# A hybrid convolution and attention layer on one core: the first three weight chunks taken k by k with the modulation, and the output product in 512 columns

## The chip, the cores and the metric

The kernel runs on one core of a Trainium2 chip. The metric is device time in microseconds (us), the median of the runs shown. A profile of one execution, taken by the hardware profiler, stands beside it; all times of single instructions are from that execution. The engines are TensorE (PE, with its weight loads as PEld), VectorE (DVE), ScalarE (ACT), GpSimd (POOL) and SyncE (SP), whose queue issues the transfers.

## What is computed

One layer over 512 latent tokens of width 1024, with 256 context tokens. Cut to what matters here:

```
sh, sc, gt = split(silu(c) @ w_mod + b_mod)        # three vectors of 1024
h  = rmsnorm(x, pre_g) * (1 + sc) + sh             # 512 x 1024
hc = rmsnorm(ctx, pre_g) * (1 + sc_c) + sh_c       # same with c_ctx
parts = split(h @ w_in)      # b, c, x_in, z_a (conv) | q, k, v, z_b (attention) | g_a, g_b
y_a = (silu(z_a) * b * conv3(c * x_in)) @ w_out_conv
y_b = (silu(z_b) * neighbourhood_attention(q, k, v, k_ctx, v_ctx)) @ w_out_attn
y = (sigmoid(g_a) * y_a + sigmoid(g_b) * y_b) @ w_o
out = x + gt * rmsnorm(y, post_g)
```

All data are float32.

## The kernel before, in words

**Split products.** Each operand of a large product is split in two parts in a shorter format, a high part H (a cast on ACT) and a low part L (a subtraction on DVE): `split`. A product is then three matmuls per k (128 of the 1024 input channels): H by H, H by the low part of the activations, L by H. `step_T` issues them (lines 107 to 109) with weights as the stationary operand and 512 tokens as columns; `proj_N` (lines 120 to 122) has the activations stationary and 256 weight columns moving.

**Weights.** They come in chunks of 1024 x 256 (two units of 128 columns). `load_chunk` reads a chunk in two halves into two `raw` buffers and splits them into `wH` and `wL`, two buffers of each. `Chunks` loads one chunk ahead of the one in use, in the order of a hand-written plan. The order in which engines take their instructions is otherwise set by a scheduler that goes by the order of the program and by when data are ready.

**First stage.** x is loaded in four tiles of 128 tokens, normed (`normed`: sum of squares on ACT, Sqrt, reciprocal and scaling on DVE), and turned on TensorE into eight tiles of 128 channels by 512 tokens, all eight PSUM banks being used; each is drained by ACT with the gain pre_g. For each k, `load_slab` loads two slabs of w_mod (each 128 x 1024, 512 KB); `condition` forms the scale and the shift of these 128 channels as two sums over a slab on DVE (line 249); `modulate` applies them on ACT in place (line 257) and splits the result into `hx`. Chunks 0 to 2 give six units with one accumulator each. `more` brings one of them in at each of k = 0, 1, 2 and `steps` then catches up on earlier k. Four of the eight k of chunk 0 are taken as float32 (line 288), the other four are split (line 291). Chunk 3 is loaded ahead at k = 6.

**Conv stage.** The first conv outputs are formed from the six accumulators, chunk 3 follows, then `conv(2)` and `conv(3)` with four more chunks (each yields after a unit). After each unit, `modulate_c` does one k of the context's modulation (two sums on DVE, two slabs of w_mod, of which those of k = 5 to 7 are still there).

**Attention, merge, output.** Attention follows with the other projections filled in between its blocks. In the merge loop (j = 0 to 7) each j takes a chunk of the two branch projections, sums them into `mg[j]`, splits it, and works out two gates for j + 2. `post_gain` runs in this loop at j = 5 to 7: it reads c again, reads the last eight slabs of w_mod, forms eight sums (line 600), and turns the result into a row `gpost` (line 612). The output stage takes w_o in four chunks of 256 columns. For each chunk and each of four token tiles come 24 matmuls, a sum of squares on ACT (line 661) and a multiplication with `gpost` on DVE (line 662). After the last chunk the norm, the residual (line 677) and the store follow.

Of the kernel before, what the change touches and what calls it, by code (L numbers as in the profile page):

```python
# [15 lines left out]
P = 128  # L16
D = 1024
# [10 lines left out]
def layer(ctx: ExitStack, tc, xp, ctxt, cc, wmod, small, win, wout, wo, rel, tab, out):  # L28
# [22 lines left out]
    nc.vector.memset(eps, EPS)  # L51
    hcv = const.tile([P, 32], F32, name="hcv")
    cosin = const.tile([P, 2, S], F32, name="cosin")

# [23 lines left out]
    def load_chunk(src, pool=wp, raws=wp):  # L78
        H = pool.tile([P, KT, 256], F32R, name="wH", bufs=2 if pool is wp else 1)
        L = pool.tile([P, KT, 256], F32R, name="wL", bufs=2 if pool is wp else 1)  # L80
        for i in range(2):
            s = slice(4 * i, 4 * i + 4)
            raw = raws.tile([P, 4, 256], F32, name="raw", bufs=2)
            nc.sync.dma_start(raw, src[:, s])
            split(H[:, s], L[:, s], raw)
        return H, L

    class Chunks:
# [5 lines left out]
        def load(self, n, *pools):  # L94
            if n < len(self.srcs) and n not in self.ahead:
                self.ahead[n] = load_chunk(self.srcs[n], *pools)
# [53 lines left out]
    order += [wo[c] for c in range(4)]  # L150
# [53 lines left out]
    with ExitStack() as p0:  # L204
# [8 lines left out]
        def normed(xt, n, vec):  # L213
            junk = st.tile([P, D], F32, name="junk")
            ss = const.tile([P, 1], F32, name=f"ss{n}")
            if vec:
                nc.vector.tensor_tensor_reduce(
                    out=junk, in0=xt, in1=xt, scale=1.0, scalar=0.0, op0=ALU.mult, op1=ALU.add, accum_out=ss
                )
            else:  # L220
                nc.scalar.activation(junk, xt, AF.Square, accum_out=ss)
            nc.scalar.activation(ss, ss, AF.Sqrt, bias=eps, scale=1.0 / D)
            nc.vector.reciprocal(ss, ss)
            nc.vector.tensor_scalar(out=xt, in0=xt, scalar1=ss, scalar2=None, op0=ALU.mult)

# [18 lines left out]
        def condition(k, v):  # L244

            cols[k, v] = st.tile([P, 2], F32, name=f"col{v}", bufs=4)
            for i in range(2):
# [12 lines left out]
        accs = Banks(5, 0, 1, 2, 3, 4)  # L260
        acc, ws = [], []

        def more(n):
            if n:
                chunk.load(n, wp)
                ws.append(chunk.ahead[n])
            else:

                w = st.tile([P, 4, 256], F32, name="w0")
                H = st.tile([P, 4, 256], F32R, name="wH0")  # L270
                L = st.tile([P, 4, 256], F32R, name="wL0")
                nc.sync.dma_start(w, chunk.srcs[0][:, :4])
                raw = wp.tile([P, 4, 256], F32, name="raw")
                nc.sync.dma_start(raw, chunk.srcs[0][:, 4:])
                split(H, L, raw)
                ws.append((w, H, L))
            acc.extend(accs() for i in range(2))

        def steps(ks, us):
            for k in ks:  # L280
                for i in us:
                    if i >= 2:
                        step_T(acc[i], ws[i // 2], i % 2, hx, k)
                        continue
                    w, H, L = ws[0]
                    cs = slice(i * P, (i + 1) * P)
                    if k < 4:
                        nc.tensor.matmul(acc[i], lhsT=w[:, k, cs], rhs=xnT[k], start=k == 0, stop=False)
                    else:
                        for lhs, rhs in ((H, hx[0][k]), (H, hx[1][k]), (L, hx[0][k])):  # L290
                            nc.tensor.matmul(
                                acc[i], lhsT=lhs[:, k - 4, cs], rhs=rhs, start=False, stop=k == KT - 1 and lhs is L
                            )


        ones = const.tile([1, P], F32, name="ones")
        nc.vector.memset(ones, 1.0)
        crow = hp.tile([1, 2, S], F32, name="crow", tag="a0")
        nc.sync.dma_start(crow, cc[0:1].rearrange("o (a n) -> o a n", a=2))
        nc.sync.dma_start(sp, small)  # L300
        xn = [load_x(xp, i, f"x{i}", f"u{i}", hp) for i in range(4)]
        load_slab(0)
        bsc1 = const.tile([P, KT], F32, name="bsc1")
        nc.vector.tensor_scalar(out=bsc1, in0=sp[:, BM + 8:BM + 16], scalar1=1.0, scalar2=None, op0=ALU.add)
        nc.vector.tensor_scalar(out=hcv, in0=sp[:, CW:CW + 32], scalar1=0.5, scalar2=None, op0=ALU.mult)
        nc.scalar.activation(crow, crow, AF.Silu)
        nc.scalar.activation(const.tile([P, 1], F32, name="dummy"), eps, AF.Sqrt)

        for i in range(2):
            ps = tps()  # L310
            nc.tensor.matmul(ps, lhsT=ones, rhs=crow[:, i], start=True, stop=True)
            nc.vector.tensor_copy(cb[:, 0, i * S:(i + 1) * S], ps)
        xnT = halves("a")
        every = Banks(7, 0, 1, 2, 3, 4, 5, 6)
        tp = [every() for k in range(KT)]
        for i in range(4):
            normed(xn[i], f"x{i}", False)
            for k in range(KT):
                nc.tensor.transpose(tp[k][:, i * P:(i + 1) * P], xn[i][:, k * P:(k + 1) * P], ident)
        condition(0, 0)  # L320

        def drained(k):
            nc.scalar.activation(xnT[k], tp[k], AF.Identity, scale=sp[:, PG + k:PG + k + 1])

        drained(0)
        u = halves("u")
        for k in range(KT):
            if k:
                load_slab(k)
                condition(k, 0)  # L330
            modulate(k, 0, xnT[k], hx[0][k], hx[1][k])
            for i in ((1, 2, 3), (4, 5, 6, 7))[k] if k < 2 else ():
                drained(i)
            if k == KT - 1:
                nc.sync.dma_start(cb[:, 1], cc[1:2].broadcast_to([P, D]))
                nc.scalar.activation(cb[:, 1], cb[:, 1], AF.Silu)
            if k < 3:
                more(k)
            if k == 6:
                chunk.load(3, st)  # L340
            steps((k,), range(min(2 * k, 6)))
            if k < 3:
                steps(range(k + 1), (2 * k, 2 * k + 1))
        chunk.n = 3
        cn = [load_x(ctxt, i, f"c{i}", f"a{2 + i}", hp) for i in range(2)]
        for i in range(2):
            normed(cn[i], f"c{i}", i % 2)
# [6 lines left out]
        for k in range(KT):  # L354
            turned(ctT[k], cn, k)
# [405 lines left out]
```

## Time and profile before

| | us |
|---|---|
| median of 3 runs | 752.48 |
| lowest, highest | 749.15, 752.82 |
| profiled execution, time | 751.83 |
| profiled execution, span (first to last instruction) | 749.9 |

The span is what the profile divides into; the time of the same execution is 1.93 us longer. An engine's busy time is not its useful work: matmuls are pipelined, so two that follow each other overlap in the records, and the distance between their starts is what one costs. A wait is the idle time of an engine ahead of an instruction, with the instruction that ended it.

### The profile page before, as it was taken

The page shows a single profiled execution, that of the slowest core. Times are in us where ns is not written, and L with a number is a line of the kernel's source. Part 1 is how long each engine was busy: PE and PEld are TensorE (multiplying, and loading weights), DVE is VectorE, ACT ScalarE, POOL GpSimd, SP SyncE. Part 2 cuts the span into 40 slices and gives each one's busy share as a digit, 9 for nine tenths or more (in the row PEclk, how much of TensorE's full clock was granted, in tenths as well). Part 3 has the DMA queues.
Part 4 walks back from the last instruction along what each step waited for, and adds up shares of the span by engine and source line. Part 5 has one row for each costly group of instructions (what it writes and reads, how often), then busy time and mean ns, then how long its engine had stood idle before and what let it go on. Part 6 is the DMA issues. An engine that isn't in the chain of part 4 may idle for free.

```text
span 749.9 us, 10146 instructions
## 1 busy us (share of the span) xinstructions
PE 728.8 (97%) x3924; PEld 623.4 (83%) x3924; DVE 508.3 (68%) x1031; ACT 333.6 (44%) x602; POOL 0.7 (0%) x6
## 2 busy tenths in 40 slices
PE   5889999999999999999999999999999999999996
PEld 3568889888889888988889988888888888888896
DVE  4778993698796977958969678675753323338434
ACT  7666442354364544534636435534722222231422
POOL 0000000000000000000000000000000000000000
PEclk9999999999999999999999999999999999999999
DMA  8883842123211221221221222222133233348413
GB/s 327 287 312 125 297 156 97 57 71 110 73 50 64 68 102 57 72 71 67 88 99 44 80 75 71 79 88 74 58 112 110 71 101 113 107 150 302 142 57 113
DMA packets 25682, 86.16 MB, mean 115 GB/s; under 512 B 2977, under 2 KB 3489, under 8 KB 25634
## 3 DMA queue, kind: packets, MB, share of 16 engines
q1 hardware_dynamic: 25634, 85.51, 33.2%
q8 instruction: 31, 0.51, 0.3%
q14 instruction: 17, 0.14, 0.1%
HBM read 83.40 MB, written 2.10 MB: 114 GB/s over the span
## 4 chain that ended last, share of the span: by engine, by line
PE 87%; DMA 5%; DVE 5%; issue 1%; SPq 1%; ACT 1%; DVEq 0%; ACTq 0%
PE ps L107 20%; PE ps L109 20%; PE ps L108 20%; PE ps L120 5%; PE ps L122 5%; PE ps L121 5%; PE ps L499 4%; PE ps L484 4%; PE ps L453 3%; DMA wm<-in_wmod 2%; DMA wg<-in_wmod 1%; DVE junk L600 1%; DVE wL L71 1%; PE ps L462 1%; DMA raw<-in_win 1%
## 5 line engine op out<-in xcount | busy, mean ns | idle before, releaser
L107 PE MATMUL ps<-h,wH 128*128 128x512 f32 x560 | 223.6, 400 | 0.0
L109 PE MATMUL ps<-h,wL 128*128 128x512 f32 x560 | 219.6, 393 | 0.0
L108 PE MATMUL ps<-h,wH 128*128 128x512 f32 x560 | 219.5, 392 | 0.0
L70 ACT CAST wH<-raw 128x1024 fp32r<-128x1024 f32 x103 | 106.7, 1050 | 158.7 <-PE ps L108 137.6
L71 DVE TENSOR_TENSOR wL<-raw,wH 128x1024 fp32r<-128x1024 f32 x103 | 125.1, 1219 | 64.8 <-ACT wH L70 60.2
L107 PEld LDWEIGHTS ps<-h,wH 128*128 128x128 f32 x560 | 105.8, 189 | 22.9 <-ACT wH L70 1.3
L109 PEld LDWEIGHTS ps<-h,wL 128*128 128x128 f32 x560 | 105.3, 188 | 23.3 <-issue 0.7
L108 PEld LDWEIGHTS ps<-h,wH 128*128 128x128 f32 x560 | 105.9, 189 | 21.5 <-DVE h L71 0.4
L476 ACT ACTIVATE pt<-ps,m 128x512 f32<-128x512 f32 x64 | 44.1, 690 | 43.8 <-DVE m L473 43.5
L469 DVE CUSTOM_DVE_ANT_1 ps<-ps,bt 128x512 f32<-128x512 f32 x56 | 38.8, 694 | 22.6 <-PE ps L453 19.3
L70 ACT CAST TH<-ps 128x512 fp32r<-128x512 f32 x64 | 37.1, 586 | 19.8 <-PE ps L484 19.5
L71 DVE TENSOR_TENSOR TL<-ps,TH 128x512 fp32r<-128x512 f32 x64 | 43.5, 681 | 0.9
L120 PE MATMUL ps<-wH,mg 128*128 128x256 f32 x128 | 37.2, 290 | 1.8 <-ACT mg L73 1.8
L484 PE MATMUL ps<-ident,pt 128*128 128x128 f32 x256 | 38.2, 272 | 0.4 <-DVE pt L478 0.4
L120 PE MATMUL ps<-wH,h 128*128 128x256 f32 x128 | 36.9, 288 | 0.0
L121 PE MATMUL ps<-wL,mg 128*128 128x256 f32 x128 | 36.9, 288 | 0.0
L122 PE MATMUL ps<-wH,mg 128*128 128x256 f32 x128 | 36.7, 288 | 0.0
L484 PEld LDWEIGHTS ps<-ident,pt 128*128 128x128 f32 x256 | 31.0, 140 | 6.6 <-issue 0.6
L121 PE MATMUL ps<-wL,h 128*128 128x256 f32 x128 | 36.2, 283 | 0.0
L122 PE MATMUL ps<-wH,h 128*128 128x256 f32 x128 | 36.2, 283 | 0.0
L631 DVE SCALAR_TENSOR_TENSOR g<-g,ps 128x512 f32<-128x512 f32 x16 | 10.9, 684 | 35.7 <-PE ps L109 35.7
L478 DVE TENSOR_SCALAR pt<-pt,z 128x512 f32<-128x512 f32 x64 | 30.9, 483 | 1.3
(158 smaller groups left out, 1257.1 us busy)
## 6 DMA issues: line engine op xcount, KB each, us to landing
raw<-in_win SPq DMA_DIRECT2D x79, 512.0 KB, 3.6
wm<-in_wmod SPq DMA_DIRECT2D x26, 512.0 KB, 7.3
raw<-in_wout SPq DMA_DIRECT2D x16, 512.0 KB, 4.5
bt<-in_rel SPq DMA_DIRECT2D x16, 256.0 KB, 2.6
wg<-in_wmod SPq DMA_DIRECT2D x8, 512.0 KB, 4.6
raw<-in_wo SPq DMA_DIRECT2D x8, 512.0 KB, 4.1
x<-in_xp SPq DMA_DIRECT2D x4, 512.0 KB, 5.2
xr<-in_xp SPq DMA_DIRECT2D x4, 512.0 KB, 8.8
```

The lines of the kernel that those rows point to most:

```text
L70: nc.scalar.copy(H, src)
L71: nc.vector.tensor_sub(L, src, H.bitcast(F32))
L107: nc.tensor.matmul(ps, lhsT=H[:, k, cs], rhs=mH[k], start=k == 0, stop=False)
L108: nc.tensor.matmul(ps, lhsT=H[:, k, cs], rhs=mL[k], start=False, stop=False)
L109: nc.tensor.matmul(ps, lhsT=L[:, k, cs], rhs=mH[k], start=False, stop=k == KT - 1)
L120: nc.tensor.matmul(ps, lhsT=mH[k][:, ts], rhs=H[:, k], start=k == 0, stop=False)
L121: nc.tensor.matmul(ps, lhsT=mH[k][:, ts], rhs=L[:, k], start=False, stop=False)
L122: nc.tensor.matmul(ps, lhsT=mL[k][:, ts], rhs=H[:, k], start=False, stop=k == KT - 1)
L469: nc.vector.tensor_tensor_reduce(out=s3, in0=s3, in1=bt[:, e::4 - e][:, 0:2], scale=1.0, scalar=-3.0e38, op0=ALU.add, op1=ALU.max, accum_o ...
L476: nc.scalar.activation(pt, s, AF.Exp, bias=m, scale=1.0, accum_out=z)
L478: nc.vector.tensor_scalar(out=pt, in0=pt, scalar1=z, scalar2=None, op0=ALU.mult)
L484: nc.tensor.transpose(tp[:, c], pt[:, c * P:(c + 1) * P], ident)
```

## The change

In the first stage, the three first chunks are stored on the host as one array `wfirst` with a slab of 128 x 768 for each k. For each k, the two slabs of w_mod and the slab of weights are loaded together, three k ahead at the most; the slab is cast and its low part taken; all six accumulators are fed from k = 0 on, 18 matmuls for each k, with no float32 product left. x is turned two k ahead into two PSUM banks, and the modulation reads it from PSUM (the gain pre_g is multiplied into the scale). The sums of squares of x alternate between ACT and DVE. The whole block is put under `manual_schedule`, which keeps the written order of instructions on PE, DVE, ACT and SP. The context's norm is moved into the block, and chunk 3 is loaded in it at k = 5.

In the conv stage, two pieces of work are done after each unit in place of one: the eight of the context's modulation, then eight sums of the post gain (`gain`), which leave `post_gain`. In the merge loop only the turning of the post gain stays, at j = 5. w_o is stored in two halves of 512 columns; the first is loaded at j = 6 into the space of `hx`, the second into the weight buffers. For the first half, k = 0 to 6 of all four token tiles come ahead of k = 7.

```diff
...
+        raws, first = {}, {}
+        def load_first(k):
...
+            nc.sync.dma_start(raws[k], wfirst[k])
+        def cast_first(k):
+            H, L = (st.tile([P, 768], F32R, name=n, bufs=3) for n in ("fH", "fL"))
+            first[k] = H, L
+            nc.scalar.copy(H, raws[k])
+        def rest_first(k):
...
+            nc.vector.tensor_sub(L, raws[k], H.bitcast(F32))
+        def turn_x(k):
+            tp = tps()
+            for t in range(4):
+                nc.tensor.transpose(tp[:, t * P:(t + 1) * P], xn[t][:, k * P:(k + 1) * P], ident)
+            return tp
+        def steps(k):
+            H, L = first.pop(k)
+            for i in range(6):
+                cs = slice(i * P, (i + 1) * P)
+                nc.tensor.matmul(acc[i], lhsT=H[:, cs], rhs=hx[0][k], start=k == 0, stop=False)
+                nc.tensor.matmul(acc[i], lhsT=L[:, cs], rhs=hx[0][k], start=False, stop=False)
+            for i in range(6):
+                cs = slice(i * P, (i + 1) * P)
+                nc.tensor.matmul(acc[i], lhsT=H[:, cs], rhs=hx[1][k], start=False, stop=k == KT - 1)
...
+        with tc.manual_schedule(engines={E.PE, E.DVE, E.Activation, E.SP}):
...
+            xn = [load_x(xp, i, f"x{i}", f"u{i}", hp) for i in range(4)]
+            for k in range(3):
+                load_slab(k)
+                load_first(k)
...
+            nc.scalar.activation(crow, crow, AF.Silu)
...
+            for i in range(2):
+                spread.append(tps())
+                nc.tensor.matmul(spread[i], lhsT=ones, rhs=crow[:, i], start=True, stop=True)
...
+            for i in range(4):
+                top = tops[:, i:i + 1]
+                if i % 2:
...
+                    nc.vector.tensor_tensor_reduce(
+                        out=junk, in0=xn[i], in1=xn[i], scale=1.0, scalar=0.0, op0=ALU.mult, op1=ALU.add, accum_out=top
+                    )
+                else:
+                    nc.scalar.activation(junk_a, xn[i], AF.Square, accum_out=top)
+                nc.scalar.activation(top, top, AF.Sqrt, bias=eps, scale=1.0 / D)
+                nc.vector.reciprocal(top, top)
+                nc.vector.tensor_scalar(out=xn[i], in0=xn[i], scalar1=top, scalar2=None, op0=ALU.mult)
+                if i < 2:
+                    nc.vector.tensor_copy(cb[:, 0, i * S:(i + 1) * S], spread[i])
+            turned_x = {k: turn_x(k) for k in range(2)}
             for k in range(KT):
+                cast_first(k)
+                if k == 0:
+                    rest_first(k)
+                    condition(k, 0, [0])
+                condition(k, 0, [1])
+                col = cols.pop((k, 0))
+                nc.vector.tensor_mul(col[:, 0:1], col[:, 0:1], sp[:, PG + k:PG + k + 1])
+                if k:
+                    rest_first(k)
+                if k + 1 < KT:
+                    condition(k + 1, 0, [0])
+                m = st.tile([P, S], F32, name="m", bufs=2)
+                nc.scalar.activation(m, turned_x.pop(k), AF.Identity, bias=col[:, 1:2], scale=col[:, 0:1])
+                split(hx[0][k], hx[1][k], m)
+                if k + 3 < KT:
+                    load_slab(k + 3)
+                    load_first(k + 3)
+                elif k == 5:
+                    chunk.load(3)
+                steps(k)
+                if k + 2 < KT:
+                    turned_x[k + 2] = turn_x(k + 2)
+            nc.sync.dma_start(cb[:, 1], cc[1:2].broadcast_to([P, D]))
+            nc.scalar.activation(cb[:, 1], cb[:, 1], AF.Silu)
+            cn = [load_x(ctxt, i, f"c{i}", f"a{2 + i}", hp) for i in range(2)]
+            for i in range(2):
...
+            for i in range(2):
...
         w = chunk()
+        pj.tags = (7, 6)
         conv_out(1, cs, unit(w, 0), unit(w, 1))
+        pj.tags = (0, 1, 2, 3, 4, 5)
...
+        def gain(k):
+            t = st.tile([P, D], F32, name="wm", bufs=6)
+            nc.sync.dma_start(t, wmod[16 + k])
...
+            nc.vector.tensor_tensor_reduce(
+                out=junk, in0=t, in1=cb[:, 0], scale=1.0, scalar=sp[:, BM + 16 + k:BM + 17 + k],
+                op0=ALU.mult, op1=ALU.add, accum_out=gains[:, k:k + 1],
+            )
         ks = [5, 6, 7, 0, 1, 2, 3, 4]
+        work = [lambda k=k: modulate_c(k) for k in ks] + [lambda k=k: gain(k) for k in range(KT)]
         for j in range(2, 4):
             for _ in conv(j):
-                if ks:
-                    modulate_c(ks.pop(0))
-        while ks:
-            modulate_c(ks.pop(0))
+                for f in work[:2]:
+                    f()
+                del work[:2]
+        for f in work:
+            f()
+        nc.vector.tensor_mul(gains, gains, sp[:, QG:QG + KT])
...
+    def load_wo(c, H, L):
+        for i in range(4):
+            raw = wp.tile([P, 2, S], F32, name="raw", bufs=2)
+            nc.sync.dma_start(raw, wo[c, :, 2 * i:2 * i + 2])
+            for k in range(2):
+                split(H[2 * i + k], L[2 * i + k], raw[:, k])
+        return H, L
...
-            gains = post_gain()
-            next(gains)
+            gpost = bp.tile([P, D], F32, name="gpost")
+            for i in range(2):
+                gb = cv.tile([P, S], F32, name="ta")
+                ps = pj()
+                for k in range(4):
+                    n = 4 * i + k
+                    nc.vector.tensor_copy(gb[:, k * P:(k + 1) * P], gains[:, n:n + 1].broadcast_to([P, P]))
+                    nc.tensor.transpose(ps[:, k * P:(k + 1) * P], gb[:, k * P:(k + 1) * P], ident)
+                nc.scalar.copy(gpost[:, i * S:(i + 1) * S], ps)
         if j == 6:
-            next(gains)
-        if j == 7:
-            gpost = next(gains)
+            t = [hp.tile([P, 2, S], F32R, name=f"wo{i}", tag=f"h{i}") for i in range(8)]
+            wos = [load_wo(0, [x[:, i] for x in t[:4] for i in range(2)], [x[:, i] for x in t[4:] for i in range(2)])]
...
+    sums = const.tile([P, 4, 3], F32, name="sums")
+    t = [[wp.tile([P, 4, S], F32R, name=n, bufs=2) for i in range(2)] for n in ("wH", "wL")]
+    wos.append(load_wo(1, *([x[:, i] for x in y for i in range(4)] for y in t)))
+    for c in range(2):
+        H, L = wos[c]
+        cs = slice(c * S, (c + 1) * S)
+        ps = [pj() for t in range(4)]
+        def steps(t, ks):
+            ts = slice(t * P, (t + 1) * P)
+            for k in ks:
+                nc.tensor.matmul(ps[t], lhsT=mm[0][k][:, ts], rhs=H[k], start=k == 0, stop=False)
+                nc.tensor.matmul(ps[t], lhsT=mm[0][k][:, ts], rhs=L[k], start=False, stop=False)
+                nc.tensor.matmul(ps[t], lhsT=mm[1][k][:, ts], rhs=H[k], start=False, stop=k == KT - 1)
+        if c == 0:
             for t in range(4):
                 nc.sync.dma_start(xr[t], xp[t * P:(t + 1) * P])
+            for t in range(4):
+                steps(t, range(KT - 1))
         for t in range(4):
+            steps(t, range(KT - 1, KT) if c == 0 else range(KT))
+            nc.scalar.activation(sq, ps[t], AF.Square, accum_out=sums[:, t, c:c + 1])
+            nc.vector.tensor_mul(ys[t][:, cs], ps[t], gpost[:, cs])
+            if c == 0:
                 nc.vector.tensor_scalar(
...
+    wfirst = np.ascontiguousarray(win[:3].transpose(2, 1, 0, 3)).reshape(8, 128, 768)
...
-    wo = chunks(units(a["w_o"][0]), list(range(8)))
+    wo = np.ascontiguousarray(a["w_o"][0].reshape(8, 128, 2, 512).transpose(2, 1, 0, 3))
```

## Rows read from the trace of the kernel before

**Rows 1.** The page, busy us of each engine, its share and instructions.
```profile
PE 728.8 (97%) x3924; PEld 623.4 (83%) x3924; DVE 508.3 (68%) x1031; ACT 333.6 (44%) x602; POOL 0.7 (0%) x6
```

**Rows 2.** Waits of TensorE: us in total, times, longest.
```profile
PE ps L288 <- ACT a L257: 3.8, 2, 2.5
...
PE ps L120 <- ACT mg L73: 1.8, 1, 1.8
```

**Rows 3.** Windows: length, busy us (count) by engine, PEclk, DMA share, GB/s.
```profile
27.00:41.00 14.00, 13.45 (x51) 9.00 (x49) 10.79 (x14) 5.18 (x7) 0.00 (x0) 1.00 0.92 334
43.00:46.80 3.80, 3.70 (x9) 2.93 (x10) 3.80 (x7) 2.61 (x4) 0.00 (x0) 0.55 1.03 379
60.90:118.00 57.10, 57.10 (x261) 46.90 (x260) 50.91 (x86) 27.25 (x44) 0.00 (x0) 1.00 0.58 194
698.50:702.10 3.60, 3.56 (x17) 3.57 (x18) 2.24 (x3) 1.42 (x3) 0.00 (x0) 0.53 0.63 221
702.10:743.80 41.70, 41.70 (x348) 41.54 (x347) 16.71 (x41) 12.59 (x36) 0.00 (x0) 1.00 0.19 66
```

**Rows 4.** Grouped lines of TensorE, 0 to 59.5 us.
```profile
L107 PE MATMUL ps<-h,wH 128*128 128x512 f32 x30 | 13.3, 455 | 0.0
...
L291 PE MATMUL ps<-h,wH 128*128 128x512 f32 x16 | 6.0, 433 | 1.9 <-DVE h L71 1.0 <-ACT h L70 0.9
```

**Rows 5.** Timeline of TensorE: start, us, engine, line, out<-in.
```profile
36.68 1.02 PE L288 MATMUL ps<-a,w 128*128 128x512 f32 x2
37.14 0.80 PE L107 MATMUL ps<-h,wH 128*128 128x512 f32 x1
37.77 0.39 PE L108 MATMUL ps<-h,wH 128*128 128x512 f32 x1
...
60.91 0.40 PE L107 MATMUL ps<-h,wH 128*128 128x512 f32 x1
...
649.62 0.39 PE L107 MATMUL ps<-us,wH 128*128 128x512 f32 x1
...
655.06 0.39 PE L107 MATMUL ps<-as,wH 128*128 128x512 f32 x1
...
693.93 0.36 PE L120 MATMUL ps<-wH,mg 128*128 128x256 f32 x1
...
743.56 0.28 PE L122 MATMUL ps<-wH,mg 128*128 128x256 f32 x1
```

**Rows 6.** Chain that ended last: start, us, what.
```profile
159.26 0.44 PE ps L484 x4
```

**Rows 7.** Timeline of ACT.
```profile
7.50 0.29 ACT L222 ACTIVATE ssx<-ssx,eps 128x1 f32<-128x1 f32 x1
```

**Rows 8.** Grouped lines, shapes apart, whole span: busy us, mean ns.
```profile
L71 DVE TENSOR_TENSOR wL<-raw,wH 128x1024 fp32r<-128x1024 f32 x103 | 125.1, 1219 | 64.8 <-ACT wH L70 60.2 <-PE ps L484 4.3
...
L249 DVE CUSTOM_DVE_ANT_0 junk<-wm,cb,sp 128x1024 f32<-128x1024 f32 x16 | 20.5, 1281 | 0.2
...
L662 DVE TENSOR_TENSOR ys<-ps,gpost 128x256 f32<-128x256 f32 x16 | 6.8, 422 | 23.2 <-ACT sq L661 23.2
...
L257 ACT ACTIVATE a<-a,col 128x512 f32<-128x512 f32 x8 | 6.5, 817 | 7.2 <-DVE col L249 7.2
...
L661 ACT ACTIVATE sq<-ps 128x256 f32<-128x256 f32 x16 | 6.1, 384 | 29.7 <-PE ps L122 29.7
...
L71 DVE TENSOR_TENSOR h<-a,h 128x512 fp32r<-128x512 f32 x8 | 5.5, 688 | 2.7 <-ACT h L70 2.7
L157 DVE TENSOR_TENSOR cs<-cs,ps 128x512 f32<-128x512 f32 x8 | 5.5, 685 | 12.9 <-PE ps L109 11.1 <-ACT cs L156 1.7
...
L70 ACT CAST h<-a 128x512 fp32r<-128x512 f32 x8 | 5.0, 620 | 0.1
...
L224 DVE TENSOR_SCALAR x<-x,ssx 128x1024 f32<-128x1024 f32 x4 | 3.0, 752 | 0.1
...
L613 ACT COPY gpost<-ps 128x512 f32<-128x512 f32 x2 | 1.1, 590 | 1.0 <-PE ps L612 1.0
```

More of the change, by code (lines that the diff above doesn't have):

```diff
@@ L27, in layer @@
 @with_exitstack
-def layer(ctx: ExitStack, tc, xp, ctxt, cc, wmod, small, win, wout, wo, rel, tab, out):
+def layer(ctx: ExitStack, tc, xp, ctxt, cc, wmod, small, wfirst, win, wout, wo, rel, tab, out):
     nc = tc.nc
@@ L242, in layer, with condition @@
         cols = {}
-        def condition(k, v):
-            cols[k, v] = st.tile([P, 2], F32, name=f"col{v}", bufs=4)
-            for i in range(2):
+        def condition(k, v, halves=(0, 1)):
+            if 0 in halves:
+                cols[k, v] = st.tile([P, 2], F32, name=f"col{v}", bufs=4)
+            for i in halves:
                 junk = st.tile([P, D], F32, name="junk")
@@ L258, in modulate @@
             split(H, L, m)
[L260 to L293, printed above, removed]
@@ L296, in layer @@
         ones = const.tile([1, P], F32, name="ones")
-        nc.vector.memset(ones, 1.0)
+        bsc1 = const.tile([P, KT], F32, name="bsc1")
         crow = hp.tile([1, 2, S], F32, name="crow", tag="a0")
[L299 to L314, printed above, removed]
@@ L315, in layer @@
-        tp = [every() for k in range(KT)]
-        for i in range(4):
-            normed(xn[i], f"x{i}", False)
-            for k in range(KT):
[L319 to L343, printed above, removed]
+        tops = const.tile([P, 4], F32, name="tops")
@@ new lines, in layer @@
+        topc = const.tile([P, 2], F32, name="topc")
+        u = halves("u")
+        acc = [pp.tile([P, S], F32, name="ps", tag=f"bank{i}") for i in range(6)]
+        raws, first = {}, {}
+        def load_first(k):
+            raws[k] = st.tile([P, 768], F32, name="fraw", bufs=3)
+            nc.sync.dma_start(raws[k], wfirst[k])
[3 more added lines that the diff above has]
+            nc.scalar.copy(H, raws[k])
@@ L650, in layer @@
     sq = bp.tile([P, S], F32, name="sq", tag="as0")
-    sums = const.tile([P, 4, 5], F32, name="sums")
-    for c in range(4):
-        w = chunk()
-        cs = slice(c * 256, (c + 1) * 256)
-        if c == 1:
+    sums = const.tile([P, 4, 3], F32, name="sums")
[12 more added lines that the diff above has]
+        if c == 0:
@@ L667, in layer @@
+            nc.scalar.activation(sq, ps[t], AF.Square, accum_out=sums[:, t, c:c + 1])
+            nc.vector.tensor_mul(ys[t][:, cs], ps[t], gpost[:, cs])
+            if c == 0:
                 nc.vector.tensor_scalar(
-                    out=b, in0=b, scalar1=1.0 / D, scalar2=EPS, op0=ALU.mult, op1=ALU.add
+                    out=sums[:, t, 2:3], in0=sums[:, t, 0:1], scalar1=1.0 / D, scalar2=EPS, op0=ALU.mult, op1=ALU.add
                 )
-            if c == 3:
-                r = sums[:, t, 3:4]
-                nc.scalar.activation(r, r, AF.Sqrt, bias=sums[:, t, 4:5], scale=1.0 / D)
+            else:
+                r = sums[:, t, 1:2]
+                nc.scalar.activation(r, r, AF.Sqrt, bias=sums[:, t, 2:3], scale=1.0 / D)
@@ L747 @@
     tab = np.ascontiguousarray(np.stack([np.cos(ang), np.sin(ang) * sign], axis=1).astype(np.float32))
-    arrays = dict(xp=xp, ctxt=a["ctx"][0], cc=cc, wmod=wmod, small=small, win=win, wout=wout, wo=wo, rel=rel, tab=tab)
+    arrays = dict(xp=xp, ctxt=a["ctx"][0], cc=cc, wmod=wmod, small=small, wfirst=wfirst, win=win, wout=wout, wo=wo, rel=rel, tab=tab)
     nc = bacc.Bacc("TRN2", target_bir_lowering=False, num_devices=1)
```

82 lines of the change are left out of this document (25 added, 57 removed).

## Prediction

> **What bounds the kernel now.** I read the page's busy table first: TensorE is busy 728.8 of 749.9 us [rows 1], so what counts is how long its stream of matmuls is and where it stands still. The list of waits, for TensorE alone, says where: the long waits lie in the first 45 us (3.8 us for the modulated x among them), plus one of 1.8 us before the output stage [rows 2]. Between these TensorE never starves, and a saving on another engine there is worth nothing. The table of stretches adds a second loss: after such waits the granted clock is 0.55 and 0.53, the 1.2 GHz level, for 3.8 and 3.6 us, and 1.00, 2.4 GHz, otherwise [rows 3]. So the reader is to look at three places: the first stage, the conv stage behind it (TensorE full, DVE busy 50.9 of 57.1 us), and the output stage with the tail.
>
> **Where the first stage ends now.** It is done when chunks 0 to 2 are. Up to 59.5 us the grouped instructions show 30 matmuls on each of lines 107, 108 and 109 (the row of 107 stands) and all 24 of line 291, sixteen of them with wH [rows 4]. Chunks 1 and 2 need 96 of lines 107 to 109, so 6 are missing; at 0.233 us each the stage ends at 60.9 us, where the timeline starts the next chunk [rows 5]. Some records can be missing from the trace; were it three, the end would be 60.2.
>
> **First stage, TensorE's work.** A split product costs three matmuls of 512 columns at about 0.23 us. The float32 product of line 288 costs more: from 36.68 to 37.77 lie one of these and one matmul of line 107 [rows 5], so 1.09 - 0.23 = 0.86 us against 0.69. Six units of eight k by three are 144 x 0.23 = 33.1 us; before it is 8 x 0.86 + 120 x 0.23 = 34.5. The x transposes (eight groups of four) now lie partly between the k steps: six groups at 0.44 us [rows 6] are 2.6 us there.
>
> **First stage, its start.** The first Sqrt runs at 7.5 us [rows 7]; I leave it there, since ACT loads two tables ahead of it either way. Then the written order alternates ACT and DVE: scale of x0 0.75, copy of c 0.69 (as line 157, a read of PSUM), sum of x1 1.28 (as line 249), Sqrt 0.29, scale 0.75, copy 0.69, scale of x2 0.75 (its square on ACT lies beside), sum of x3 1.28, Sqrt 0.29, scale 0.75 [rows 8]. With 0.29 for the first Sqrt, some 0.16 for four reciprocals and small handoffs, x3 is scaled at 16.2. DVE goes on with the low part of the first weight slab, 0.75 x 1.22 = 0.91, two sums of 1.28 and a small multiply 0.15: 19.9. ACT modulates (0.82 as line 257, though from PSUM, where line 613 takes 0.59) and rounds (0.62) [rows 8]: TensorE starts k = 0 at about 21.4. It has stood still before that, so I charge one stretch at the lower clock like that from 43.0 to 46.8, which at 0.55 loses 1.7 us [rows 3]. End: 21.4 + 1.7 + 33.1 + 2.6 = 58.8, rounded up to 59.1 for handoffs. Against 60.9 that is **-1.8 us**. Bounds: full clock from the first step and a start half a us earlier give 56.6 (-4.3); nothing gained is 0; a stage that the queues hold up is priced with the rivals.
>
> **What could hold the k steps up.** DVE per k: two sums 2.56, multiply 0.15, low part of the slab 0.91, low part of h 0.69 [rows 8], together 4.3 us, against TensorE's 18 x 0.23 + 0.44 = 4.6. The order of the block is fixed on PE, DVE, ACT and SP, and a sum for k + 1 stands ahead of the low part of h for k; if its slab is late, the last six matmuls of step k wait. The split of chunk 3 stands in the same queue behind k = 5: two subtractions of 1.22 on DVE [rows 8]. Seven intervals of 4.3 and these 2.4 put the last modulation column at 19.9 + 32.5 = 52.4, h at 53.9, the last matmul at 53.9 + 4.1 = 58.0: DVE is 1.1 us short of setting the end. The transfers: x is 2.1 MB, each k 1.05 MB of w_mod and 0.39 MB of wfirst, in all 13.6 MB; at 334 GB/s [rows 3] they take 41 us, so k = 7 is there at about 43, ahead of use. SP issues k + 3 when the slots of k come free, so three sets are in flight. I cost the queues at nothing; their cover is TensorE's own backlog of about 1 us.
>
> **Conv stage.** Its modulation of the context goes two per unit, and the eight sums of the post gain (8 x 1.28 = 10.2 us on DVE) move here from the merge stage, where TensorE waited for none of them. With them SP issues 18 slab loads here instead of ten, through the same six slots; one that waits for its slot, which DVE frees, holds the raw weights queued behind it. DVE is busy 50.9 of 57.1 us here [rows 3]; with them 61.1, that is 4.0 us more than the stretch holds. But the two norms of the context have moved ahead, as has the second half of chunk 3's split, and DVE is free from about 54 to 59, when chunk 4 can be split already; later splits have the value stage behind them. I take 0; the bounds are 0 and +4.0, if all of it came to stand ahead of a weight split. Nothing is gained here, as TensorE is full.
>
> **Output stage.** Now 384 matmuls of 256 columns: 348 records in 41.7 us are 0.12 each [rows 3], and from 693.93 to 743.69 [rows 5] the stage takes 49.8 us, of which 46.1 are matmuls and the rest the wait of 1.8 us for mg [rows 2] and its 3.6 us at 0.53, which lose 1.7 [rows 3]. After: 192 of 512 columns. The same shape takes 0.2267 in the merge stage, where 24 of them lie between 649.62 and 655.06 [rows 5], so 43.5 us: **-6.3 us**, of which 2.6 is fewer matmuls and 3.6 the wait and its clock. The wait is covered because 84 matmuls (k below 7, four tiles, 19 us) come first, and mg's last part came at 698.5, 4.6 us after the stage's start. At 0.233, the spacing that the missing six above would have at the most, it is 44.7: -5.1. What is late next is w_o itself: eight casts of 0.62 and eight subtractions of 0.69 for each half [rows 8]; h is free after the last gate, some 22 us ahead, and two raw slots turn it round in about 14. The gpost transposes move in front of this, at equal price.
>
> A rule stands against part of that. The Trainium skill, TensorE: Matmul & The Clock Gate, section "Back-to-back issue gap", puts the fixed cost of a matmul at full clock at about 2.5 ns, whatever its width. By that page 384 narrow matmuls take an estimated 41.9 us and 192 wide ones 41.4, so fewer matmuls would be worth 0.5 us, not 2.6, and the stage -4.1. The trace does not agree: its 0.12 and 0.2267 us leave 13.5 ns per matmul saved, and the measurement decides.
>
> **Tail.** The last square grows from 0.38 (256 columns) to about 0.59 (a 512-column read of PSUM, line 613), the multiply from 0.42 to 0.69 [rows 8]: **+0.5 us**; what follows keeps its shapes. Bounds +0.2 (one of them hidden) and +0.5.
>
> **Sum.** -1.8 + 0 - 6.3 + 0.5 = -7.6 us. The profiled execution's span of 749.9 becomes 742.3, and its time of 751.83, 1.93 more than the span, 744.2. The median of the runs, 752.48, is 0.65 above it: 744.9, said as 745.
>
> **Rivals.** (a) The first stage gains nothing: the front chain or DVE's queue eats 1.8 us. For it: only 1.1 us between DVE and TensorE. Time 747. (b) Conv stage: DVE is late with the low parts of weights and TensorE waits up to 4.0 us; 749. For it: DVE's 89% there; against it: the early start of chunk 4. (c) The slower side: TensorE waits for data ahead of each k step and begins each at 1.2 GHz. One such stretch costs 1.7 us [rows 3]; eight, of which one is counted, cost 11.9 more: 757. Five further slow steps cancel the forecast's gain, and only all seven make it slower by more than 0.5%. Against it: a step that starts low takes longer than its data needs, so that the next finds its data there. The Trainium skill, same page, section "HAM oscillation — how this bites in real kernels", tells of a kernel in which waits between groups of matmuls brought every group to half clock; the dips after waits agree, the trace shows no such series. (d) More than forecast: full clock from the first step, 742.
>
> **Chances.** Forecast 0.60 (743 to 747), (a) 0.14, (b) 0.13, (c) 0.06, (d) 0.07. A measurement of this kernel can tell about 0.5% from no change, that is 3.8 us: 748.7 and below is faster. Faster: 0.60 + 0.14 + 0.07 = 0.81; same: (b), 0.13; slower: (c), 0.06. Range: from (d) with the lower bound of the start, 741, to (b) with a smaller gain of the output stage, 750.5; outside it remain (c) and some of the edges, under 2 in 10.
>
> **What would show it.** TensorE's waits: none of 1.8 us ahead of the output stage, and few after 22 us. First matmul of k = 0 at 21.4 and the last of k = 7 at 59.1; 192 wide matmuls in 43.5 us; last matmul to end of span 6.7 us. Wrong if DVE's low part of h or the sums end TensorE's waits after k = 3, if the conv stage shows waits for wL, or if 512 columns against w_o run slower than against h.

## The result, and the profile after

The changed kernel takes 742.94 us (median of 4 runs, 742.77 to 743.47), the kernel before 750.82 beside it: a ratio of 0.9908, interval 0.9880 to 0.9936. Forecast were 745.0 us and a ratio of 0.990. The profiled execution has a span of 741.7 us and a time of 743.47.

The page's first line, which answers to [rows 1]: TensorE's stream has become 7.8 us shorter, and its share has stayed.

```profile
PE 721.0 (97%) x3740; PEld 612.3 (83%) x3740; DVE 507.8 (68%) x1027; ACT 323.4 (44%) x583; POOL 0.7 (0%) x6
```

TensorE's waits in the changed kernel (us in total, times, longest), beside [rows 2]:

```profile
PE ps L273 <- DVE x L321: 4.9, 3, 2.0
PE ps L280 <- ACT h L70: 3.7, 1, 3.7
PE ps L308 <- DVE hcv L299: 3.2, 1, 3.2
PE ps L273 <- DVE cb L323: 1.1, 1, 1.1
PE ps L479 <- DVE ks L458: 0.4, 1, 0.4
PE ps L510 <- DVE pt L504: 0.4, 1, 0.4
```

The first four end by 19.42 us, when k = 0 starts. After that only two waits of 0.4 us are left in attention; the one for `mg` is gone.

The windows of the changed kernel, columns as in [rows 3]: k = 0, then k = 1 to 7, the conv stage, the output stage.

```profile
19.40:26.40 7.00, 6.98 (x18) 5.55 (x19) 7.00 (x13) 2.83 (x4) 0.00 (x0) 1.00 1.03 406
...
26.40:57.20 30.80, 30.80 (x148) 25.28 (x147) 25.28 (x40) 18.24 (x23) 0.00 (x0) 1.00 0.81 287
57.20:115.00 57.80, 57.80 (x264) 47.27 (x263) 56.53 (x97) 28.28 (x48) 0.00 (x0) 1.00 0.74 248
...
691.07:734.60 43.53, 43.53 (x193) 35.85 (x191) 15.32 (x29) 10.97 (x25) 0.00 (x0) 1.00 0.23 85
```

TensorE is busy throughout in all four, but in the first its 18 matmuls stand 0.4 us apart. DVE is busy 56.5 of 57.8 us in the conv stage (50.9 of 57.1 before [rows 3]), and TensorE waits for it nowhere there.

The timeline of TensorE in the changed kernel, beside [rows 5]; lines 280 to 284 are the k steps, lines 677 to 679 the output stage:

```profile
19.42 0.80 PE L280 MATMUL ps<-h,fH 128*128 128x512 f32 x1 [3.67 <-ACT h L70]
20.01 0.63 PE L281 MATMUL ps<-h,fL 128*128 128x512 f32 x1
20.44 0.63 PE L280 MATMUL ps<-h,fH 128*128 128x512 f32 x1
...
26.44 0.60 PE L273 MATMUL ps<-ident,x 128*128 128x128 f32 x4
...
54.55 0.39 PE L107 MATMUL ps<-h,wH 128*128 128x512 f32 x1
...
58.03 1.52 PE L284 MATMUL ps<-h,fH 128*128 128x512 f32 x6
59.39 0.39 PE L107 MATMUL ps<-h,wH 128*128 128x512 f32 x1
...
691.07 0.39 PE L677 MATMUL ps<-wo,mg 128*128 128x512 f32 x1
...
734.36 0.39 PE L679 MATMUL ps<-wH,mg 128*128 128x512 f32 x1
```

The first stage ends at 59.39 us. But six matmuls of chunk 3 already lie among its steps (three from 49.65 us, three from 54.55 us), 1.36 us of work that belongs behind it, so it is worth an end at 58.0. From there to the output stage 633.1 us pass, as many as before (60.91 to 693.93, 633.0 [rows 5]). So the 8.2 us between the two spans split cleanly: 2.9 in the first stage, 6.3 in the output stage (49.8 before [rows 5], 43.5 now), 0.1 given back between them and 0.9 in the tail (6.2 before, 7.1 now).

### The profile page after: what moved, and what is told of

Read it like the earlier page. It is cut to its first block, busy times and chain, and to the rows that moved or that the text cites. A ratio compares the mean times of both kernels' runs of the same rounds, so it can differ in the third digit from the quotient of the medians.

```text
span 741.7 us, 9770 instructions
## 1 busy us (share of the span) xinstructions
PE 721.0 (97%) x3740; PEld 612.3 (83%) x3740; DVE 507.8 (68%) x1027; ACT 323.4 (44%) x583; POOL 0.7 (0%) x6
## 4 chain that ended last, share of the span: by engine, by line
PE 93%; DVE 4%; ACT 1%; issue 1%; DMA 0%; DVEq 0%; ACTq 0%
PE ps L107 20%; PE ps L109 20%; PE ps L108 20%; PE ps L525 4%; PE ps L510 4%; PE ps L120 3%; PE ps L479 3%; PE ps L122 3%; PE ps L121 3%; PE ps L678 2%; PE ps L677 2%; PE ps L679 2%; PE ps L280 2%; PE ps L281 2%; PE ps L284 2%; PE ps L488 1%
## 5 line engine op out<-in xcount | busy, mean ns | idle before, releaser
L107 PE MATMUL ps<-h,wH 128*128 128x512 f32 x528 | 209.5, 397 | 0.0
L108 PE MATMUL ps<-h,wH 128*128 128x512 f32 x528 | 206.3, 391 | 0.0
L109 PE MATMUL ps<-h,wL 128*128 128x512 f32 x528 | 206.2, 391 | 0.0
L70 ACT CAST wH<-raw 128x1024 fp32r<-128x1024 f32 (+1 forms) x98 | 98.1, 1016 | 152.5 <-PE ps L108 132.7
L71 DVE TENSOR_TENSOR wL<-raw,wH 128x1024 fp32r<-128x1024 f32 (+1 forms) x98 | 114.6, 1175 | 65.3 <-ACT wH L70 60.8
L109 PEld LDWEIGHTS ps<-h,wL 128*128 128x128 f32 x528 | 99.1, 188 | 21.0
L108 PEld LDWEIGHTS ps<-h,wH 128*128 128x128 f32 x528 | 99.3, 188 | 19.3
L107 PEld LDWEIGHTS ps<-h,wH 128*128 128x128 f32 x528 | 99.2, 188 | 19.2
L71 DVE TENSOR_TENSOR TL<-ps,TH 128x512 fp32r<-128x512 f32 x64 | 43.5, 681 | 0.9
L525 PE MATMUL ps<-TH,V 128*128 128x256 f32 (+1 forms) x96 | 28.5, 319 | 0.0
L446 ACT ACTIVATE qd<-ta 64x512 fp32r<-64x512 f32 x32 | 20.2, 630 | 17.7 <-PE ps L488 9.6
L525 PE MATMUL ps<-TL,V 128*128 128x256 f32 (+1 forms) x96 | 27.8, 319 | 0.0
```

The costliest lines, as they stand in the source:

```text
L70: nc.scalar.copy(H, src)
L71: nc.vector.tensor_sub(L, src, H.bitcast(F32))
L107: nc.tensor.matmul(ps, lhsT=H[:, k, cs], rhs=mH[k], start=k == 0, stop=False)
L108: nc.tensor.matmul(ps, lhsT=H[:, k, cs], rhs=mL[k], start=False, stop=False)
L109: nc.tensor.matmul(ps, lhsT=L[:, k, cs], rhs=mH[k], start=False, stop=k == KT - 1)
L525: nc.tensor.matmul(o3[:, dst], lhsT=V[p][:, kt, h], rhs=src(t), start=n == 0 and t is TH, stop=n == len(work) - 1 and t is TL,)
```

## The experiments

The medians of the kernel before, taken beside these runs, lie between 749.16 and 751.38 us, and variants of the changed kernel are compared with its 742.94. The first k step of the changed kernel varies: in its profiled execution and in those of five variants that leave this step alone it ended between 25.3 and 26.4 us, because the matmuls change from a spacing of 0.43 us to 0.23 at different places in it. A span or a median by itself therefore tells nothing under about 1 us; lengths of stages do.

**The old output stage in the changed kernel.** The four chunks of 256 columns are back, the post gain stays in the conv stage.

```diff
-    for c in range(2):
-        H, L = wos[c]
...
+    for c in range(4):
+        w = chunk()
+        cs = slice(c * 256, (c + 1) * 256)
...
+            ps = pj()[:, :256]
+            proj_N(ps, w, mm, slice(t * P, (t + 1) * P))
```

> The changed kernel with the old output stage (four chunks of 256 columns of w_o, each tile's k in turn); all else as changed. Theory of the prediction: 384 matmuls at 0.12 us, the wait of 1.8 us for mg and its 3.6 us at the lower clock come back, less 0.5 to 0.9 of tail: 5.4 to 5.8 us more than the changed kernel's 742.9, so 748.5. Rival: the wait in the old stage came from the post gain's work in the merge loop, which is gone here; then only the matmul count comes back, 2.6 less the tail: 745.

744.13 us (743.98 to 744.33). The stage takes 46.2 us, 2.7 more than in the changed kernel, with no wait for `mg`; the tail is 0.8 shorter. So the 3.6 us of the wait and its clock do not come back with the old stage: what made `mg` late for it is gone from the kernel.

**The post gain alone moved, in the kernel before.**

```diff
+        work = [lambda k=k: modulate_c(k) for k in ks] + [lambda k=k: gain(k) for k in range(KT)]
...
+                for f in work[:2]:
+                    f()
+                del work[:2]
...
-            gains = post_gain()
-            next(gains)
```

> The kernel before with one part of the change alone: the eight sums of the post gain go to the conv stage, two pieces of work after each unit, and only the turning of the gain stays in the merge loop. First stage and output stage are the old ones. Theory, formed after the run with the old output stage: the wait of 1.8 us for mg and the 3.6 us at the lower clock came from the post gain's transfers and sums in the merge loop, so both go without any change of the output stage: 3.6 us less than the kernel before, about 746.5. Rival, as the prediction had it: the wait is the chain behind mg and only the order of k covers it; then it stays and the time is that of before, 750.

746.67 us (746.25 to 747.47; 749.16 before beside it, ratio 0.9963, 0.9949 to 0.9978). The windows of this kernel's output stage:

```profile
692.66:696.30 3.64, 3.64 (x30) 3.51 (x29) 3.40 (x5) 2.53 (x3) 0.00 (x0) 1.00 0.08 32
696.30:738.90 42.60, 42.60 (x357) 42.56 (x355) 17.28 (x41) 13.06 (x38) 0.00 (x0) 1.00 0.22 75
```

With the old stage and the old order TensorE is full from its first microsecond and at full clock, 46.2 us in place of 49.8: moving the gain's sums out of the merge loop, and with them their eight transfers and the second reading of c, removes the wait for `mg` by itself. The chain that ended last in the kernel before (start, us, what) shows how they had made it late:

```profile
683.37 6.26 DMA wg<-in_wmod
...
689.65 1.28 DVE junk L600
...
691.15 1.15 DVE wL L71
...
692.36 4.47 DMA raw<-in_wo
...
696.91 1.04 ACT wH L70
697.95 0.54 ACT mg L73
...
698.53 0.50 PE ps L120
```

The last sum of the gain waits for its slab, the subtraction that frees a `raw` buffer stands behind it on DVE, the next transfer of w_o starts only then, and the rounding of `mg` stands on ACT behind the cast of that transfer.

**k = 7 in turn.** The first half of the output takes its k in order.

```diff
-            for t in range(4):
-                steps(t, range(KT - 1))
         for t in range(4):
-            steps(t, range(KT - 1, KT) if c == 0 else range(KT))
+            steps(t, range(KT))
```

> The changed kernel without the reordering in the first half of w_o: k = 7 is taken in turn in each token tile. Theory of the prediction: the wait for the last mg (1.8 us) and its low clock (1.7) come back: 746.4. Rival: with 512 columns the 21 matmuls ahead of k = 7 take 4.8 us in place of 2.5, which covers the last mg already; then no wait and 742.9.

743.92 us (743.82 to 745.42), 1.0 more. The timeline of TensorE shows where it waits, 5 us into the stage:

```profile
695.09 0.39 PE L679 MATMUL ps<-wo,mg 128*128 128x512 f32 x1
695.85 0.50 PE L677 MATMUL ps<-wo,mg 128*128 128x512 f32 x1 [0.37 <-ACT mg L73]
```

The stage takes 44.5 us, 1.0 more. The new order is worth 1.0 us here, not 3.6. That it is worth anything has a cause of its own. In the changed kernel the rounding of the last part of `mg` starts 4.6 us into the stage (3.9 before), because the splits of the wide w_o slabs now stand ahead of it, as the timelines of DVE and of ACT in that kernel show:

```profile
693.00 1.29 DVE L71 TENSOR_TENSOR wL<-raw,wH 128x512 fp32r<-128x512 f32 x2 [2.16 <-ACT wH L70]
694.21 0.68 DVE L638 SCALAR_TENSOR_TENSOR g<-g,ps 128x512 f32<-128x512 f32 x1
...
695.65 0.63 ACT L73 ACTIVATE mg<-g 128x512 fp32r<-128x512 f32 x1 [2.16 <-DVE g L641]
```

**Narrow matmuls in the new stage.** Each output matmul becomes two of 256 columns. The accumulation is changed with it, so that the sums are not those of the layer: the run stands for its time alone.

```diff
+                for n in range(2):
+                    ns = slice(n * 256, (n + 1) * 256)
...
+                    nc.tensor.matmul(ps[t][:, ns], lhsT=mm[0][k][:, ts], rhs=H[k][:, ns], start=k == 0, stop=False, **one)
```

> The changed kernel with each matmul of the output stage cut into two of 256 columns, all else the same. By the rows (0.12 against 0.2267 us) 384 narrow matmuls cost 2.6 us more than 192 wide ones: 745.5. By the fixed cost of about 2.5 ns per matmul that the Trainium skill states (TensorE: Matmul & The Clock Gate, Back-to-back issue gap) it would be 0.5 us: 743.4.

745.15 us (745.10 to 745.84), 2.2 more, and the window of this kernel's stage is 46.07 us against 43.53:

```profile
690.17:736.24 46.07, 46.07 (x385) 46.02 (x383) 15.34 (x29) 10.98 (x25) 0.00 (x0) 1.00 0.22 81
```

2.5 us over 192 further matmuls is 13 ns each; the old stage with its 384 narrow matmuls, 46.2 us in the first run above, agrees. The Trainium skill (TensorE: Matmul & The Clock Gate, "Back-to-back issue gap") gives its 2.5 ns for the gap of an isolated matmul; the estimate of 0.5 us that the prediction worked out from it is not what this stream of weight loads and matmuls shows.

**The old first stage in the changed kernel.** `more`, `steps` over earlier k and the float32 half chunk are back, without the fixed order.

```diff
-        with tc.manual_schedule(engines={E.PE, E.DVE, E.Activation, E.SP}):
...
+        def more(n):
+            if n:
+                chunk.load(n, wp)
+                ws.append(chunk.ahead[n])
```

> The changed kernel with the old first stage (three chunks brought in one by one, four k of chunk 0 in float32, no fixed order); conv stage, merge and output as changed. Theory: the first stage is worth the 2.9 us that the two traces show, so 745.8. Rival: the old first stage loses no more, since the conv stage behind it fills TensorE anyway and a later start is made up there: 743. Rival on the other side: with the gain's eight sums and without the early split of chunk 4, DVE runs late in the conv stage and TensorE waits: over 748.

744.97 us (744.63 to 746.04), 2.0 more; the output stage starts 2.0 later (693.04). TensorE's waits in the k steps are nearly those of before again:

```profile
PE ps L288 <- ACT a L257: 3.8, 2, 2.5
PE ps L291 <- ACT h L71: 1.3, 1, 1.3
...
PE ps L291 <- DVE h L72: 1.0, 1, 1.0
```

**More DVE work per k step.** The low part of each weight slab is formed twice, 0.95 us per k.

```diff
-            nc.vector.tensor_sub(L, raws[k], H.bitcast(F32))
+            for _ in range(2):
+                nc.vector.tensor_sub(L, raws[k], H.bitcast(F32))
```

> The changed kernel with the low part of each k's weight slab formed twice: 0.9 us more on DVE for each k, 7 in all. By the prediction DVE is 1.1 us short of setting the end: 6 more, 749. By the trace after, DVE is idle for 5.5 of the 30.8 us between 26.4 and 57.2: 1.5 more, 744.5. If the order of the queue has more play than that: 743.

746.16 us (745.70 to 747.60), 3.2 more by the medians. k = 0 starts 1.5 us later, at 20.93, and one wait in the k steps is new:

```profile
52.24 0.50 PE L107 MATMUL ps<-h,wH 128*128 128x512 f32 x1 [1.75 <-ACT m L340]
```

In this execution, the fastest of its seven, k = 0 took 6.1 us in place of 7.0, and with that the two account for about 2.4 us; its span is 2.2 longer than that of the changed kernel. The rest of the 3.2 is not traced. The other seven doubled operations, 6.6 us of DVE work, cost TensorE the one wait of 1.75. DVE was idle for 5.5 us between 26.40 and 57.20 in the changed kernel (its window above), and here twelve matmuls of chunk 3, in place of six, have moved in between the k steps and fill part of what TensorE would have waited.

**More DVE work in the conv stage.** Each sum of the post gain is formed twice, 10.3 us.

```diff
+            for _ in range(2):
+                nc.vector.tensor_tensor_reduce(
```

> The changed kernel with each of the eight sums of the post gain formed twice: 10.3 us more on DVE in the conv stage, which is 56.5 of 57.8 us busy there. If DVE holds TensorE up once it is full (the prediction's case b): 747 to 753. If the weight splits keep ahead and the value stage takes up the rest: 743.

743.43 us (743.14 to 745.32), 0.5 more, with one new wait of TensorE:

```profile
PE ps L107 <- DVE V L71: 1.1, 1, 1.1
```

The 0.5 us is within what the first k step varies by; the wait is what the trace shows. Ten further microseconds of DVE work cost about one at the most, so the moved sums themselves had room behind that stage.

**TensorE busy before k = 0.** Five float32 matmuls on data of no use stand between the first transposes.

```diff
+            def busy(i, n):
+                nc.tensor.matmul(acc[5][:, :n], lhsT=ident, rhs=xn[i][:, :n], start=True, stop=True)
...
+                if t < 3:
+                    busy(t, (512, 256, 512)[t])
+            turned_x = {0: tp0, 1: turn_x(1)}
+            for i in range(2):
+                busy(i, 512)
```

> The changed kernel with five float32 matmuls of x by the identity put between the transposes of x, into a bank that k = 0 overwrites: TensorE does not stand still ahead of k = 0. Theory: k = 0 then runs at 2.4 GHz and saves up to the 2.9 us that its 18 matmuls lose now: 740.5. Rival: the queue of DVE, held by the split of chunk 3 behind k = 5, sets the time of k = 6 and 7, and TensorE waits there for what it gained: 742 to 743.

742.87 us (742.51 to 743.14): no gain by the medians. The timeline of TensorE shows that the cause was met, k = 0 being done in 4.3 us in place of 7.0, and that waits come back in its place, at 47.41 and 53.03 us (the 2.51 at the top lies ahead of k = 0 and is not new):

```profile
19.54 0.50 PE L280 MATMUL ps<-h,fH 128*128 128x512 f32 x1 [2.51 <-ACT h L70]
...
23.80 0.60 PE L273 MATMUL ps<-ident,x 128*128 128x128 f32 x4
...
47.41 0.50 PE L107 MATMUL ps<-h,wH 128*128 128x512 f32 x1 [0.18 <-ACT m L349]
...
53.03 0.50 PE L280 MATMUL ps<-h,fH 128*128 128x512 f32 x1 [0.60 <-ACT h L70]
...
57.28 0.39 PE L107 MATMUL ps<-h,wH 128*128 128x512 f32 x1
```

From the end of k = 0 to the end of k = 7, without the one matmul of chunk 3 among the steps, 33.25 us pass (23.80 to 57.28, less 0.23), against 31.59 in the changed kernel (26.44 to 59.39, less 1.36): 1.7 of the time saved in k = 0 is lost again there.

The timeline of DVE in the same kernel names what is late: its queue stands at chunk 3's low part, which needs ACT's cast of a transfer still under way, and a sum of the modulation is queued behind it.

```profile
42.69 2.52 DVE L71 TENSOR_TENSOR wL<-raw,wH 128x1024 fp32r<-128x1024 f32 x2 [2.39 <-ACT wH L70]
45.13 1.28 DVE L236 CUSTOM_DVE_ANT_0 junk<-wm,cb,sp 128x1024 f32<-128x1024 f32 x1
```

**Chunk 3 one k step later, with and without the busy start.**

```diff
-                elif k == 5:
+                elif k == 6:
                     chunk.load(3)
```

> The busy start of the run before, and chunk 3's split behind k = 6 in place of k = 5, so that DVE's queue does not stand 2.4 us for its transfer ahead of the sums of k = 6. Theory: this standing is what took back the 2.6 us that the busy start saved in k = 0; with both, 740.5. Rival: DVE's own work per k holds TensorE, wherever the split stands; 742.9.

> The changed kernel with chunk 3's split behind k = 6 and no busy start. Theory: TensorE is behind DVE here, as k = 0 began at the lower clock, so the queue's wait costs nothing: 742.9. Rival: the queue's wait already costs TensorE something in k = 6 and 7, which the early matmuls of chunk 3 conceal: 742 or less.

With the busy start 741.40 us (740.79 to 741.62), 1.5 less than the busy start alone: DVE's stand before chunk 3 had held the gain back. The steps behind k = 0 take 31.48 us here (23.73 to 55.89, less 0.68), as in the changed kernel. The 740.5 that were expected are missed by 0.9; the trace has one new wait of that length behind the stage, in the turning of the context (that it is the same 0.9 is not shown):

```profile
PE ps L218 <- ACT ctT L219: 0.9, 1, 0.9
```

Without the busy start 741.89 (741.70 to 742.23), 1.05 less than the changed kernel, which looks as if the stand cost 1 us there too. The traces don't bear that out. From the end of k = 0 to the end of k = 7, without chunk 3's own matmuls, pass 31.47 us (25.33 to 56.80) here and 31.59 in the changed kernel; what is earlier in this execution is the end of k = 0, by the 1.1 us by which that varies. Whether moving the load alone gains anything stays open.

**Without the fixed order.**

```diff
-        with tc.manual_schedule(engines={E.PE, E.DVE, E.Activation, E.SP}):
+        if True:
```

> The changed kernel without the fixed order of the first stage; the scheduler orders it. If the fixed order carries the first stage's gain: back to the 745 of the run with the old first stage, or over. If the even feeding of six accumulators carries it: 743.

740.97 us (739.50 to 741.16), 2.0 less than with it; ratio to the kernel before 0.9883 (0.9862 to 0.9903), an interval that overlaps that of the changed kernel. The timeline of TensorE:

```profile
18.05 0.78 PE L280 MATMUL ps<-h,fH 128*128 128x512 f32 x1
...
55.62 0.39 PE L107 MATMUL ps<-h,wH 128*128 128x512 f32 x1
```

The stage ends at 55.6 us, 2.4 earlier than the 58.0. Of that 1.4 is the start, 0.5 a shorter k = 0, which varies anyhow, and 0.6 the steps behind it, where one group of x transposes fewer is left (five, not six). The timeline of DVE tells why the start is earlier:

```profile
12.27 1.26 DVE L236 CUSTOM_DVE_ANT_0 junk<-wm,cb,bsc 128x1024 f32<-128x1024 f32 x1
...
13.46 0.75 DVE L321 TENSOR_SCALAR x<-x,tops 128x1024 f32<-128x1024 f32 x1
```

The first sum of the modulation runs at 12.27, ahead of the scaling of the last x tile. In the written order it stands behind that scaling and the low part of the slab, at 15.15.

**The best of these together.** No fixed order, the busy start, chunk 3 one k later.

```diff
-        with tc.manual_schedule(engines={E.PE, E.DVE, E.Activation, E.SP}):
+        if True:
...
+            for i in range(2):
+                busy(i, 512)
...
-                elif k == 5:
+                elif k == 6:
```

> The changed kernel without the fixed order, with the five float32 matmuls on data of no use between the turned x tiles, and the fourth chunk's split loaded one k step later. Theory: the two causes are separate. The free order alone took 2.0 us off (740.97), though its first twelve matmuls are still spaced 0.43 us, which costs 12 x 0.2 = 2.4 us; with the clock up from the first k step most of that goes too: 739.0 us, spacing 0.23 us in k=0 and the last h,fH matmul at about 52.5 us. Rival: the first stage is then held by VectorE's work per k, which the free order already runs without a gap, and TensorE waits for it in the later k steps: 740.5 to 741.5 us, last h,fH matmul at 54 us or later.

738.76 us (738.47 to 740.39; 751.38 before beside it, ratio 0.9840, 0.9818 to 0.9862). The timeline of TensorE:

```profile
18.04 0.50 PE L280 MATMUL ps<-h,fH 128*128 128x512 f32 x1
...
53.28 0.39 PE L107 MATMUL ps<-h,wH 128*128 128x512 f32 x1
```

The stage ends 2.3 us earlier again, about as forecast, and TensorE has no wait in the k steps. The difference lies in k = 0: 4.3 us here (18.04 to 22.30), 6.5 without the busy start.

## Why the prediction was right, and where it was not

The time (745.0 against 742.94) and the places of the gain held, and none of the signs of being wrong appears: TensorE has no wait after k = 3 of the first stage, none for wL in the conv stage, and 512 columns against w_o are spaced 0.2267 us as forecast. Of the terms not all held, and one move was credited with nothing that was worth a wait.

**First stage, -1.8 forecast, -2.9 in the traces, 2.0 by undoing it.** Two terms were mis-sized in opposite directions. k = 0 started at 19.42 us, not 21.4. I had left the first Sqrt at 7.5 us, "since ACT loads two tables ahead of it either way". That was misread: the timeline of ACT in the kernel before has three loads ahead of it, the last between the first square and the Sqrt,

```profile
6.21 1.28 ACT L222 ACT_TABLE_LOAD   x1
```

and the changed kernel, which takes the Silu first and a Sqrt of no use behind it, has two, both ahead of the first square:

```profile
0.73 1.28 ACT L302 ACT_TABLE_LOAD   x1 [0.73 <-PEq L777]
...
3.44 1.28 ACT L304 ACT_TABLE_LOAD   x1
...
6.12 0.29 ACT L319 ACTIVATE tops<-tops,eps 128x1 f32<-128x1 f32 x1
```

That is 1.4 us earlier (7.50 before [rows 7]); 0.5 more lies in the chain from there to the last scaled x tile, 8.2 us in place of 8.7. And the slow stretch, which I took for 1.7 us from another stretch, held the whole of k = 0: 7.02 us against 18 x 0.23, a loss of 2.9 (1.5 to 2.9 over the executions seen). That the two errors cancel in part is luck. The rest was right: k = 1 to 7 with their transposes were put at 29.0 + 2.6 = 31.6 us and took 31.6. Rival (d), full clock from the first step, is what the busy start brought about; by itself it did not pay. Its price was mis-added besides: the 1.7 us of the stretch off 745 give 743.3, not 742. Rival (c), every step at the low clock, is refuted: the steps follow each other every 4.57 us without a wait. So the series that the Trainium skill tells of (TensorE: Matmul & The Clock Gate, "HAM oscillation — how this bites in real kernels") does not arise here.

**What holds the k steps up.** DVE's chain was sized well: its last modulation column was put at 52.4 us and is multiplied at 52.51. But "DVE is 1.1 us short of setting the end" makes it sound stiffer than it is: 6.6 us of DVE work in the later steps cost TensorE 1.75. And "I cost the queues at nothing" was right only with the slow first step in front: in the changed kernel too DVE stands 2.0 us for chunk 3's cast, hidden by the time lost in k = 0.

**Conv stage, 0 forecast, 0.1 measured for all that lies between the two stages.** Rival (b) falls: even with twice the gain's sums TensorE has one new wait of 1.1 us.

**Output stage, -6.3 forecast, -6.3 measured, with one cause overlooked.** The 2.6 us for fewer, wider matmuls hold (2.5 by the stage, 2.2 by the medians when they are made narrow again). "The wait is covered because 84 matmuls come first" holds in the changed kernel, where the last `mg` is rounded 4.6 us into the stage and costs 1.0 us without the new order. What I overlooked is why `mg` was late: in the kernel before it was the post gain's transfers and sums, so the move that I costed at nothing gained takes the whole 3.6 us off the old stage by itself. The new stage then makes `mg` late again by its own loading of w_o, at less cost, since the 21 wide matmuls ahead of the first k = 7 already take 4.8 us. That the sum came out to the tenth owes something to luck, as either of two parts of the change takes the wait away. The new order with the gain in its old place was not run.

**Tail, +0.5 forecast, +0.9 measured.** The two wider operations run as priced (0.60 and 0.69), and from the end of the last matmul to the start of the last residual 1.7 us pass in place of 1.2. The other 0.4 us lies behind the last DVE operation, from whose end to the end of the span 3.3 us pass before and 3.7 now; what lengthens that was not tried.

The parts undone one by one give 2.0 (first stage), 1.2 (output stage) and, by its ratio, 2.8 (the gain), 6.0 of 6.9 us by the ratio: they add up within what the intervals allow, though the parts are not independent, as the wait for `mg` shows.

## What to carry to other kernels

Work that is moved off an engine's queue for one reason can free another wait: look at what stood behind it in its old place before costing the move at nothing, and look whether the new stage makes a wait of its own. Removing a loss at the start of a stage pays only as far as the next queue follows; find out what stands behind the slack that the loss provided. A written order is worth trying against none, since here the new data flow carried the gain, and the order gave some 2 us of it back.

## What the runs showed of the hardware

The granted clock is given as 1.00 from 19.40 to 26.40 us, while matmuls of 512 columns start every 0.43 us in it and every 0.23 right behind. In the kernel before, the stretch with a granted clock of 0.55 [rows 3] has the same distance, as the timeline of TensorE shows:

```profile
43.55 0.63 PE L291 MATMUL ps<-h,wL 128*128 128x512 f32 x1
43.98 0.63 PE L291 MATMUL ps<-h,wH 128*128 128x512 f32 x1
```

So at this start after idling the distance of the matmuls, not the clock's column, tells the 1.2 GHz level. With the five matmuls put before it, the same step takes 4.3 us, 0.23 us a matmul from its second on, although the transfers are as dense (DMA share 1.03 in both windows of k = 0): they are not what spaces the matmuls.

A wait of TensorE can be made by a queue several steps away: the 1.8 us for `mg` end a chain of a transfer, a sum and a subtraction on DVE, a second transfer and a cast on ACT, 15 us long.
